# Loading the weight sums earlier, and two moved steps in the mixer, in a two-layer hybrid decoder

## The chip, the cores and the metric

The kernel runs on one NeuronCore of a Trainium2 chip. The metric is the device time of one execution in microseconds (us). The engines are TensorE (PE, matrix products; its weight loads are listed as PEld), VectorE (DVE), ScalarE (ACT), GpSimd (POOL) and SyncE (SP, which here only issues DMAs).

## The reference

The program computes a decoder trunk of two layers for 256 tokens of width 2048, all in float32. Layer 0 mixes with one input projection whose columns feed an mLSTM group (8 heads) and a Mamba-2 SSD group (32 heads); layer 1 is attention with rotary positions (with 256 tokens there is one block, so only the causal part is left). Each layer ends in a SwiGLU feed-forward part with 5632 hidden columns.

```
for layer in range(2):
    xn = rms_norm(x, norm_mix[layer])
    x = x + (mixer_mlstm_ssd if layer == 0 else mixer_moba)(xn, ...)
    x = x + swiglu(rms_norm(x, norm_ffn[layer]), gate, up, down)
return rms_norm(x, final_norm)

# mLSTM part of the mixer, per head, after the chunks are put together:
#   num = (q k^T * decay) v ; nq = its row sums ; hm = num / max(|nq|, exp(-m))
#   hm  = rms_norm(hm) * sigmoid(o)
```

## The kernel before

**Products.** Every large product is a `block`: 256 tokens (two tiles of 128) by two strips of 512 output columns, summed over pairs of 128 input rows. Pair j of a block covers 256 rows. Each float32 number is split into a high and a low part, so that one product becomes three matmuls (`add`, lines 303 to 305): high times high, high times low, low times high. The letter of a plan says how a pair is done. P is the plain way, 8 products of 3 matmuls. S is Strassen's way with 7 products, 3 matmuls each, for which sums of weights and of activations are needed. PPPSPSSP, for instance, has S at pairs 3, 5 and 6. It is the plan of the blocks `v0`, `o` (twice), `qk1`, `v1`, both halves of `w2` and nearly all of layer 1's projections; most hidden blocks of the feed-forward part have PSPSPSSP.

**Weights.** `weights` (line 251) loads a pair's raw weights through SP (lines 262, 264, 266; 512 KB or 256 KB each) into one of six `raw` buffers, which hold three pairs. For an S pair it also fills a `sums` tile, one of two buffers: two plain loads of 256 KB on SP (line 260), then two accumulating loads on POOL (line 261), each of which has to wait for its plain load. Then ACT casts the high parts (line 270, `wh`, six buffers) and DVE takes the low parts (line 275, `wl`, six buffers) and two more sums (lines 285 and 287). An S pair has four casts: its first raw tile, `sums`, the second raw tile, and half of a fourth tile. The casts are tied to each other in the order of the program (`last`, `cast`) and stand at high priority (offset 800).

**Order.** The program is written as a stream; a planner then puts each engine's instructions into a fixed order, by priority (the place in the program, or earlier with `high_priority`) among what it reckons to be ready, including free buffers. On the chip every engine runs its own list in order and waits at an instruction whose inputs are not there. `tied(x)` (lines 151 to 155) puts what is traced in it behind instruction `x` on `x`'s engine. `issued` collects the first raw load of each pair, so `issued[-2]` at pair j is that of pair j - 2, since pair j's own is added afterwards.

**Later work.** Small steps between the products are put into a list by `later(wait, name, fn, ...)` and run at a `tick`, one at the end of each pair of a block; `wait` counts ticks. From the first S pair on the ticks are held back until the last S pair is through, so that in PPPSPSSP only the ticks behind pairs 0, 1 and 2, and then the one behind pair 7, run such steps. `need(name)` runs what is left under a name. Steps that come up at one tick run in the order in which they were put into the list. The auxiliary results go to the PSUM banks 7, 6, 4, 5 in turn (`aux_bank`); the same four banks hold the `acc_e` sums of the S pairs, and the first of these that a pair writes is in bank 4.

**The mixer.** After the query-key block `qk0` and the first output projection `w1` come `v0`, `o0`, and the second half, `qk1`, `v1`, `o1`, then the output projection `w2` in two halves. `qk_done` turns queries and keys with `qk_pair` (eight transposes each time, four times). `mlstm_scores` multiplies them by the decays (line 803 on DVE). In the output-gate block `o`, `mlstm_out` (products `p_num`, line 814, and copies on ACT, line 817) and `mlstm_norm` (squares on ACT, a power on POOL, scaling on ACT) run for two groups of heads, `s` = 2g and 2g + 1. At the end of the block line 851 on DVE multiplies the gate in, and `transpose_split` (line 215) turns the result, `p_tr<-ident,pre`, one block later. In layer 1 the rotary products (lines 981 to 987) and their transposes `p_qt<-ident,rot` (line 770) stand in the same relation.

## Time and profile before

| what | value |
|---|---|
| median of 3 runs | 2567.66 us (2567.1 to 2573.02) |
| the profiled execution's own time | 2568.26 us |
| its span | 2566.5 us |
| mean granted clock of PE | 0.995 |
| PE busy | 2535.6 us, 99% |
| DVE busy | 2237.1 us, 87% |
| ACT busy | 1600.2 us, 62% |
| POOL busy | 366.2 us, 14% |
| read from HBM | 627.07 MB, 245 GB/s over the span |

Busy shares are of the span. Matmuls are pipelined, so that a busy PE is not PE at its best pace. A group's row names line, engine, operation, out<-in, count, then busy time and the mean of one in ns, then the engine's idle time just before and what ended it. Lines ending in `q` after the engine's name are of its sequencer, for SP the issue of a DMA. All times within the span are in us from its start.

### The profile page before, as it was taken

How to read it: one execution, taken by the hardware profiler on the slowest of the kernel's cores; microseconds unless marked ns; L12 is line 12 of the kernel's file. 1: busy time of each engine (PE TensorE's matmuls, PEld its weight loads, DVE VectorE, ACT ScalarE, POOL GpSimd, SP SyncE). 2: the span in 40 equal slices, each digit the busy share in tenths (PEclk: the TensorE clock that was granted, in tenths of full speed). 3: DMA queues.
4: the chain of work that ended last, by engine and by line, in shares of the span. 5: the costliest groups of instructions: out<-in, count | busy, mean ns of one | idle time of the engine just before them, and what ended most of it. 6: DMA issues, size and time to landing. Idle time of an engine off the chain costs nothing.

```text
span 2566.5 us, 34451 instructions
## 1 busy us (share of the span) xinstructions
PE 2535.6 (99%) x11553; PEld 2088.3 (81%) x11553; DVE 2237.1 (87%) x2978; ACT 1600.2 (62%) x2160; POOL 366.2 (14%) x452
## 2 busy tenths in 40 slices
PE   9999999999999999999999999999999999999998
PEld 8888888878778888888888887778888888888887
DVE  6877788778789999999999988878899999999998
ACT  6566765566667665566666665656666656665665
POOL 2101111111101111111111010110011111111110
PEclk9999999999999999999999999999999999999999
DMA  8656678778768999999999887785699999999995
GB/s 281 182 172 182 212 205 257 222 220 248 225 200 261 275 274 279 280 275 273 273 291 273 253 240 212 227 233 179 192 266 273 279 282 269 285 262 293 288 267 179
DMA packets 333665, 631.51 MB, mean 246 GB/s; under 512 B 27256, under 2 KB 29824, under 8 KB 333488
## 3 DMA queue, kind: packets, MB, share of 16 engines
q1 hardware_dynamic: 278928, 527.71, 60.9%
q0 software_dynamic: 53376, 99.76, 22.7%
q8 instruction: 91, 1.49, 0.2%
q10 hardware_dynamic: 1184, 1.84, 0.2%
q14 instruction: 86, 0.70, 0.1%
HBM read 627.07 MB, written 2.14 MB: 245 GB/s over the span
## 4 chain that ended last, share of the span: by engine, by line
PE 71%; DVE 3%; DMA 2%; ACT 1%; issue 1%; POOL 0%; POOLq 0%; DVEq 0%; ACTq 0%; SPq 0%
PE acc_f L303 17%; PE acc_f L305 17%; PE acc_f L304 17%; PE acc_e L303 6%; PE acc_e L305 5%; PE acc_e L304 5%; DVE wl L275 2%; PE p_tr L215 1%; DMA sums<-in_l_w_qkv 1%; ACT wh L270 1%; DMA sums<-in_l_w_in 1%; PE p_qt L770 0%; DMA raw<-in_l_ffn_down 0%; DMA sums<-in_l_w_out 0%; PE p_o L1038 0%
## 5 line engine op out<-in xcount | busy, mean ns | idle before, releaser
L270 ACT CAST wh<-raw 128x1024 fp32r<-128x1024 f32 (+1 forms) x1084 | 1047.0, 982 | 597.7 <-PE acc_f L305 272.0
L275 DVE TENSOR_TENSOR wl<-raw,wh 128x1024 fp32r<-128x1024 f32 (+1 forms) x1084 | 1210.6, 1135 | 180.1 <-ACT wh L270 163.4
L303 PE MATMUL acc_f<-wh,x 128*128 128x512 f32 x1168 | 458.4, 392 | 0.0
L304 PE MATMUL acc_f<-wl,x 128*128 128x512 f32 x1168 | 457.8, 392 | 0.0
L305 PE MATMUL acc_f<-wh,x 128*128 128x512 f32 x1168 | 457.8, 392 | 0.0
L270 ACT CAST wh<-sums 128x1024 fp32r<-128x1024 f32 x174 | 183.0, 1052 | 199.1 <-PE acc_f L305 83.6
L303 PE MATMUL acc_f<-wh,xa 128*128 128x512 f32 x678 | 269.6, 398 | 0.7 <-ACT wh L145 0.7
L304 PE MATMUL acc_f<-wl,xa 128*128 128x512 f32 x678 | 264.8, 390 | 1.1 <-DVE wl L275 1.1
L305 PE MATMUL acc_f<-wh,xa 128*128 128x512 f32 x678 | 264.9, 391 | 0.0
L304 PEld LDWEIGHTS acc_f<-wl,x 128*128 128x128 f32 x1168 | 220.3, 189 | 45.0
L303 PEld LDWEIGHTS acc_f<-wh,x 128*128 128x128 f32 x1168 | 220.3, 189 | 44.8
L305 PEld LDWEIGHTS acc_f<-wh,x 128*128 128x128 f32 x1168 | 220.0, 188 | 45.1
L275 DVE TENSOR_TENSOR wl<-sums,wh 128x1024 fp32r<-128x1024 f32 x174 | 212.1, 1219 | 43.5 <-ACT wh L270 43.1
L303 PE MATMUL acc_e<-wh,sk 128*128 128x512 f32 x522 | 206.7, 396 | 0.1
L304 PE MATMUL acc_e<-wl,sk 128*128 128x512 f32 x522 | 204.0, 391 | 0.0
L305 PE MATMUL acc_e<-wh,sk 128*128 128x512 f32 x522 | 202.8, 390 | 0.0
L261 POOL DMA_DIRECT2D sums<-in_l_ffn_gate x86 | 74.4, 865 | 726.5 <-DMA sums<-in_l_ffn_up 278.2
L304 PEld LDWEIGHTS acc_f<-wl,xa 128*128 128x128 f32 x678 | 127.5, 188 | 27.4 <-DVE wl L275 1.9
L305 PEld LDWEIGHTS acc_f<-wh,xa 128*128 128x128 f32 x678 | 127.3, 188 | 27.1
L303 PEld LDWEIGHTS acc_f<-wh,xa 128*128 128x128 f32 x678 | 127.4, 188 | 25.7 <-ACT wh L145 0.9
L285 DVE TENSOR_TENSOR raw<-raw,sums 128x512 f32<-128x512 f32 x174 | 119.0, 684 | 25.9 <-DMA sums<-in_l_w_qkv 8.6
L261 POOL DMA_DIRECT2D sums<-in_l_ffn_down x80 | 69.9, 946 | 380.0 <-DMA sums<-in_l_ffn_down 204.0
(336 smaller groups left out, 4111.7 us busy)
## 6 DMA issues: line engine op xcount, KB each, us to landing
raw<-in_l_w_in SPq DMA_DIRECT2D x177, 512.0 KB, 4.4
raw<-in_l_ffn_gate SPq DMA_DIRECT2D x176, 512.0 KB, 6.1
raw<-in_l_ffn_down SPq DMA_DIRECT2D x136, 512.0 KB, 6.6
raw<-in_l_ffn_up SPq DMA_DIRECT2D x90, 512.0 KB, 6.4
sums<-in_l_ffn_up SPq DMA_DIRECT2D x172, 256.0 KB, 5.3
raw<-in_l_w_qkv SPq DMA_DIRECT2D x78, 512.0 KB, 5.0
raw<-in_l_w_out SPq DMA_DIRECT2D x52, 512.0 KB, 5.1
raw<-in_l_ffn_up SPq DMA_DIRECT2D x86, 256.0 KB, 5.9
```

What stands on the lines that cost most here:

```text
L215: turned = nc.tensor.transpose(pt[:, i * T + t * P:i * T + (t + 1) * P], src[t][:, i * P:(i + 1) * P], ident)
L261: nc.gpsimd.dma_start(sums[:, i, :], other, accum_op=OP.add)
L270: cast[0] = nc.scalar.copy(h[:, :n, :], of[:, :n, :]).ins
L275: last[0] = nc.vector.tensor_sub(l[:, :n, :], of[:, :n, :], h[:, :n, :].bitcast(F32)).ins
L285: nc.vector.tensor_add(b[:, 1, :], b[:, 0, :], sums[:, 0, :])
L303: nc.tensor.matmul(dst, ah, bh, start=start, stop=False, **kw)
L304: nc.tensor.matmul(dst, ah, bl, start=False, stop=False, **kw)
L305: nth[0] = nc.tensor.matmul(dst, al, bh, start=False, stop=stop, **kw).ins
```

## The change

The loads of a pair's `sums` are tied to the first raw load five pairs back in place of two. Where the query-key block has S pairs (`qk1`), all four `qk_pair` steps come up at the second tick; before, the queries came up at the first and the keys at the second. In the second output-gate block (g = 1) `mlstm_out` comes up at ticks 2 and 3 (before: 1 and 2), and `mlstm_norm` twice at tick 3 (before: 2 and 3). With g = 0 nothing changes there.

```
@@ weights
         if summed:
             sums = home("sum")([P, 2, STRIP], "sums")
-            with tied(issued[-2]):
+            with tied(issued[-5]):
                 for i, other in enumerate((unit(wa, row + P, ca), unit(wb, row, cb))):
                     nc.sync.dma_start(sums[:, i, :], unit(wb, row + P, cb))
                     nc.gpsimd.dma_start(sums[:, i, :], other, accum_op=OP.add)
@@ qk_done
             for j in range(2):
-                later(1 + i, ("qk", g), qk_pair, qk[g, i][:, 2 * j:2 * j + 2, :],
+                later(1 + i if got[1] is None else 2, ("qk", g), qk_pair, qk[g, i][:, 2 * j:2 * j + 2, :],
                       [tok[i, t][:, j * T:(j + 1) * T] for t in range(NT)])
@@ o_block
         for i in range(2):
-            later(1 + i, ("hm", g), mlstm_out, 2 * g + i)
-            later(2 + i, ("hm", g), mlstm_norm, 2 * g + i)
+            later(1 + g + i, ("hm", g), mlstm_out, 2 * g + i)
+            later(min(2 + g + i, 3), ("hm", g), mlstm_norm, 2 * g + i)
```

## The prediction

> **What bounds the kernel now.** I read the page first, for the span and the busy shares. TensorE (PE) is busy for nearly the whole span, so a change of the loading order can only win the moments in which PE stands idle or runs at a reduced clock. To find them I asked for the busy time in stretches, cut at the blocks of the mixer of layer 0 and of the projections of layer 1, which are the consecutive blocks with the plan PPPSPSSP.

> ```profile
> span 2566.5 us, 34451 instructions
> ```

> ```profile
> core 0: us, PE busy (x) PEld busy (x) DVE busy (x) ACT busy (x) POOL busy (x), PEclk, DMA share, GB/s
> 497.00:543.00 46.00, 44.16 (x191) 35.25 (x190) 29.05 (x42) 29.77 (x55) 5.53 (x6) 1.00 0.68 193
> 543.00:592.00 49.00, 45.65 (x202) 37.13 (x201) 40.21 (x50) 32.71 (x48) 8.61 (x13) 0.97 0.85 251
> ...
> 637.00:687.00 50.00, 48.97 (x219) 40.29 (x218) 35.54 (x50) 33.90 (x60) 7.30 (x9) 1.00 0.74 214
> 687.00:738.00 51.00, 45.93 (x187) 36.30 (x186) 38.72 (x56) 29.25 (x40) 4.85 (x6) 0.90 0.64 187
> ...
> 1556.00:1606.00 50.00, 46.16 (x207) 37.75 (x206) 42.22 (x58) 27.60 (x41) 5.24 (x6) 0.97 0.73 211
> 1606.00:1659.00 53.00, 51.17 (x245) 41.52 (x245) 46.35 (x73) 33.04 (x60) 5.23 (x6) 1.00 0.71 206
> 1659.00:1707.00 48.00, 46.92 (x219) 38.74 (x218) 36.31 (x51) 29.85 (x48) 5.27 (x6) 1.00 0.77 222
> 1707.00:1756.00 49.00, 46.47 (x209) 37.97 (x208) 42.42 (x59) 26.60 (x40) 5.20 (x6) 0.97 0.75 218
> sum 529.00, PE 508.44 PEld 415.50 DVE 421.68 ACT 325.89 POOL 63.25; mean PE 46.22 PEld 37.77 DVE 38.33 ACT 29.63 POOL 5.75
> ```

> The first two numbers of a row are its length and PE's busy time; the last three the granted clock, the DMA share and GB/s. The rows are, in order, the first output-gate block (o0), the second query-key block (qk1), the second output-gate block (o1), the first half of the last mixer projection (w2a), and in layer 1 aq1, av1, aq2 and aq3. The sum row covers eleven stretches: 529.00 - 508.44 = 20.56 us idle, and the eight quoted rows hold all of it (1.84, 3.35, 1.03, 5.07, 3.84, 1.83, 1.08, 2.53). Four rows show a clock below 1.00.

> The chain of waits tells what PE stood for in qk1 (start, length, what).

> ```profile
> 545.15 9.08 DMA sums<-in_l_w_in
> 554.33 1.05 ACT wh L270
> 555.41 1.23 DVE wl L275
> 556.63 0.60 DVE raw L287
> 557.24 1.21 DVE pre L851 x2
> 558.49 3.48 PE p_tr L215 x15
> ```

> An accumulating load of `sums` of pair 3 (S) lands at 554.23; ScalarE (ACT) then casts it, VectorE (DVE) takes the low part, and only then comes to L851, the gate of the block before, for which PE's transposes wait. PE did not wait for weights: it waited for other work queued on DVE behind the late `sums`. The waits and PE's groups say the same of the other blocks.

> ```profile
> ACT wh L270 <- PE acc_f L305: 355.7, 246, 6.4
> ...
> ACT wh L270 <- DMA sums<-in_l_w_in: 18.9, 4, 6.6
> ...
> ACT wh L270 <- DMA sums<-in_l_w_qkv: 14.8, 3, 6.0
> ...
> ACT wh L270 <- DMA sums<-in_l_w_out: 7.9, 2, 5.3
> ```

> ```profile
> L814 PE MATMUL p_num<-v,rows 128*128 128x257 f32 x48 | 11.5, 383 | 1.0 <-DVE rows L803 1.0
> L1038 PE MATMUL p_o<-pT,av 128*128 128x256 f32 x32 | 9.8, 389 | 1.8 <-DVE prob L1012 1.8
> L770 PE MATMUL p_qt<-ident,rot 128*128 128x128 f32 x64 | 9.8, 285 | 6.4 <-DVE rot L987 6.4
> ...
> L215 PE MATMUL p_tr<-ident,pre 128*128 128x128 f32 x32 | 7.3, 379 | 6.3 <-DVE pre L851 6.3
> ```

> The last numbers are PE's idle time before the group. 6.4 us of p_qt are aq1 and aq3 (3.84 + 2.53), 6.3 of p_tr are qk1 and 2.95 of w2a's 5.07, p_o's 1.8 is av1, p_num's 1.0 is o1. All wait for small DVE operations, in blocks where `sums` came late by 5 to 7 us at worst. The first waits row says that casts mostly wait for PE to give buffers back: weights are otherwise ahead.

> **Part 1, the tie of the sums.** Nothing is added or removed; two loads on SP and two accumulating loads on POOL per S pair may be issued earlier. Is there a free buffer? There are two, taken in turn, so pair 3 gets the one of pair 5 of the block before, which is free after that pair's low part.

> ```profile
> 527.18 1.22 DVE L275 TENSOR_TENSOR wl<-sums,wh 128x1024 fp32r<-128x1024 f32 x1
> ```

> ```profile
> 529.56 0.37 SPq L262 DMA_DIRECT2D raw<-in_l_w_in  x1
> ...
> 538.22 0.92 SPq L260 DMA_DIRECT2D sums<-in_l_w_in  x2
> ...
> 541.06 0.39 SPq L260 DMA_DIRECT2D sums<-in_l_w_in  x1
> ```

> The buffer is free at 528.40 but its loads go out at 538.22, behind the raw loads of pairs 0 to 2; the old tie is to pair 1. The new one is to pair 6 of the block before, long issued. I expect the loads at about 528.4, just ahead of raw pair 0 at 529.56: 538.22 - 528.40 = 9.8 us earlier, in a stretch with little in flight. From issue to landing it took 554.23 - 538.22 = 16.0 us; from 528.4 that is 544.4. The chain's 6.6 us longest wait is then gone, since the wait ran up to 554.33 and so began at 547.7, later than 544.4. L851 ends 6.6 us earlier, 558.45 - 6.6 = 551.9, before PE comes to its transposes (3.35 us idle before about 558.5, so 555): the whole stall goes. The same shift of 5 to 6 us in w2a, aq1 and aq3 exceeds their stalls of 2.95, 3.84 and 2.53, so these go too, and with them the 1.83 of av1 and 1.08 of aq2. Pair 5 moves from 541.06 to ahead of raw pair 1. Pair 6 waits for pair 3's buffer and not for the tie, so it only follows pair 3. On POOL each accumulation waits for its SP load to land; behind it in that queue stand the memset of v and the power operations, which no PE group above waits for, so I put this at 0.

> A stall also costs clock.

> ```profile
> 498.06 0.39 PE L304 MATMUL acc_f<-wl,xa 128*128 128x512 f32 x1
> 498.29 0.39 PE L305 MATMUL acc_f<-wh,xa 128*128 128x512 f32 x1
> ```

> ```profile
> 704.35 0.63 PE L304 MATMUL acc_f<-wl,mx 128*128 128x512 f32 x1
> 704.78 0.63 PE L305 MATMUL acc_f<-wh,mx 128*128 128x512 f32 x1
> ```

> Matmuls start 0.23 us apart before a stall and 0.43 after it. From the clock column, 0.03 x 49 + 0.10 x 51 + 0.03 x 50 + 0.03 x 49 = 9.5 us of full clock are withheld. What falls into the idle itself costs nothing, so the loss is 0 to 9.5; I take 7, near the top, since the slow starts come after the idle. [...]

> Ceiling: 20.6 + 7 = 27.6 us. Not all is due to late sums. The rest of w2a's idle, 5.07 - 2.95 = 2.1, lies later in the block, and o0's 1.84 is at S pairs behind normalising work on ACT; earlier sums give ACT room, and I take half of each (0 to all): 1.05 and 0.9 stay.

> **What is pushed back.** Raw pairs 1 and 2 now come behind pair 5's sums, 1 MB of reads in all. At the 251 GB/s of qk1 that is 4.2 us at most, in eight blocks 34 us if all of it reached PE; the other end is 0. I take 0, because PE is not near its weights there: the first waits row has 246 casts waiting for PE, while the sums rows have 9 waits. If that cover were gone, each us that raw pair 1 is later than the lead would be a us of PE idle.

> In the feed-forward blocks (PSPSPSSP) the buffers bind pairs 1, 5 and 6, and only pair 3 moves, from behind raw pair 1 to ahead of it.

> ```profile
> 860.20 0.39 SPq L260 DMA_DIRECT2D sums<-in_l_ffn_up  x1
> ```

> ```profile
> 864.61 1.06 ACT L270 CAST wh<-raw 128x1024 fp32r<-128x1024 f32 x1 [0.46 <-DMA raw<-in_l_ffn_gate]
> ```

> ```profile
> 867.91 1.22 DVE L275 TENSOR_TENSOR wl<-raw,wh 128x1024 fp32r<-128x1024 f32 x1
> ```

> There raw pair 1 is cast the moment it lands, so 0.5 MB ahead of it (about 2 us at 251 GB/s) delays the cast by 0 to 2 us. DVE takes it up at 867.91, 2.2 us after the cast ends at 865.67: covered. I take 0.

> **Part 2, queries and keys of qk1 at one tick.** Eight transposes and two ACT copies go from behind pair 0 of v1 to behind pair 1. The scores need them only after pair 2, and v1 stood without idle, since the eight quoted rows hold all idle of the sum. Cost 0; at worst the scores wait for the two extra copies.

> **Part 3, heads of o1 a pair later.** The products of s = 2 go behind pair 1, those of s = 3 behind pair 2, directly ahead of S pair 3; both normalisations come at pair 2's tick. PE's 1.03 us wait for L803 goes (in the ceiling already). New is that `acc_e` of pair 3 takes bank 4, which the products of s = 3 have just filled: its second product, three matmuls or 0.7 us after them, waits for ACT's copies.

> ```profile
> 653.46 2.76 PE L814 MATMUL p_num<-v,rows 128*128 128x257 f32 x12
> ```

> ```profile
> 656.42 1.18 ACT L817 COPY v<-p_num 128x257 f32<-128x257 f32 x4
> ...
> 660.29 1.03 ACT L270 CAST wh<-raw 128x1024 fp32r<-128x1024 f32 x1
> ```

> The four copies take 1.18 us after the products (653.46 + 2.76 = 656.22), so this wait is 0 to 1.2 on a free ACT, and up to 3.9 if copies and squares (656.42 to 660.29) stand before it; I take 1. The cast of pair 4 stands behind the squares of s = 3, which are now a pair later: 0 to 3.9, I take 1.5, like o0's 1.84. Together 2.5 us lost. POOL's small power operation of each normalisation stands behind pair 6's accumulations, as now; these come earlier with pair 3.

> Sum: 27.6 - 1.05 - 0.9 - 2.5 = 23.2 us. The profiled execution took 2568.26; 2568.26 - 23.2 = 2545.1. The median of the runs, 2567.66, is 0.6 lower, which I leave aside: 2545.

> **The rivals.** (a) Raw loads take the sums' place.

> ```profile
> raw<-in_l_w_in SPq DMA_DIRECT2D x177, 512.0 KB, 4.4
> ```

> An accumulation of 256 KB took 9.08 us where a raw load of 512 KB takes 4.4: loads in company are slow. If raw pairs 1 and 2 become as late as the accumulations (4.7 us), DVE waits there, and about half the shift is lost: 12 us gained, 2556. For it: DMA is at 0.85 in qk1; against: casts wait for PE. [...]

> (b) The order does not move. The planner goes by program order when slots are free in its own reckoning; if it still puts pair 3's sums behind raw pair 2, only part 3 acts, +2.5 - 1.0: about 2570. Against it: the sums at 541.06 already go out ahead of raw loads that stand before them in the program.

> (c) Slower. In the 20 hidden blocks of the feed-forward with the plan PSPSPSSP raw pair 1 comes so late that PE waits. If PE loses all of the 2 us, 40 us go against 23 gained: 2585. It decides from 23 / 20 = 1.2 us a block. Against it: DVE takes the cast up only 2.2 us later, as shown.

> **How the numbers follow.** Forecast (2536 to 2553) 0.65; (a) 0.13; (b) 0.12; (c) 0.10. About 0.3%, 7.7 us, is what a measurement here can tell from no change, so faster means below 2560: 0.65 + 0.10 of (a) = 0.75; the same: 0.03 + 0.12 = 0.15; slower: 0.10. The range 2536 to 2564 leaves out (c), half of (b) and 0.04 below. Its low end is the full ceiling with 9.5 for the clock, 2568.3 - 30.1 = 2538, and 2 us beside.

> **What would show it.** SP issues pair 3's sums ahead of raw pair 0; ACT's waits for sums of w_in, w_qkv and w_out fall from 41.6 us to a few; p_tr<-pre and p_qt<-rot lose their 6.3 and 6.4 us of idle; the four clock values return to 1.00; o1 shows a short wait of `acc_e` for ACT L817. The prediction is wrong if ACT's or DVE's waits for raw rise by as much, or if PE shows new idle in the feed-forward.

## The result and the profile after

The changed kernel takes 2549.89 us, the median of four runs, against 2567.38 us for the kernel before on the same chip: ratio 0.9925, 95% interval 0.9906 to 0.9945. (One of the four, at 3621 us with a granted clock of 0.654, was disturbed; the other three took 2548.43 to 2550.68, median 2549.11, and the ratio leaves it out.) The time lies inside the predicted range, about 5 us above the predicted 2545. The profiled execution took 2548.43.

```profile
span 2546.7 us, 34498 instructions
```

The span is 2566.5 - 2546.7 = 19.8 us shorter. The stretches of the prediction, cut at the same blocks (o0, qk1, o1, w2a, aq1, av1, aq2, aq3; PE's busy time, then clock, DMA share and GB/s at the end):

```profile
core 0: us, PE busy (x) PEld busy (x) DVE busy (x) ACT busy (x) POOL busy (x), PEclk, DMA share, GB/s
500.00:546.00 46.00, 46.00 (x206) 38.35 (x205) 33.74 (x46) 31.48 (x57) 7.87 (x8) 1.00 0.73 214
546.00:595.00 49.00, 47.81 (x218) 39.18 (x217) 42.84 (x54) 35.83 (x52) 8.37 (x12) 1.00 0.92 275
640.00:690.00 50.00, 50.00 (x223) 41.63 (x222) 36.20 (x50) 32.95 (x59) 7.33 (x8) 1.00 0.74 216
690.00:741.00 51.00, 47.41 (x216) 37.73 (x215) 45.13 (x65) 33.59 (x51) 5.24 (x6) 1.00 0.77 220
...
sum 396.00, PE 391.22 PEld 321.50 DVE 337.38 ACT 259.62 POOL 46.34; mean PE 48.90 PEld 40.19 DVE 42.17 ACT 32.45 POOL 5.79
```

The sum covers eight rows; the four not shown are those of layer 1, where PE is busy throughout. Of the 20.56 us idle in these blocks 396.00 - 391.22 = 4.78 are left: 1.19 in qk1 and 3.59 in w2a. Every row grants the full clock. That makes 20.56 - 4.78 = 15.8 us of idle gone, and with it up to 9.5 us of withheld clock. The sum, 25.3, is more than the span lost, so something else was paid. It stands in PE's groups, where each group's last numbers are its idle time and what ended it:

```profile
L814 PE MATMUL p_num<-v,rows 128*128 128x257 f32 x48 | 11.0, 380 | 0.0
L1038 PE MATMUL p_o<-pT,av 128*128 128x256 f32 x32 | 9.7, 384 | 0.0
L770 PE MATMUL p_qt<-ident,rot 128*128 128x128 f32 x64 | 9.4, 277 | 0.0
L699 PE MATMUL p_xs<-ident,xs 128*128 128x128 f32 x32 | 5.4, 294 | 5.6 <-DVE xs L481 5.6
L215 PE MATMUL p_tr<-ident,pre 128*128 128x128 f32 x32 | 5.2, 285 | 2.7 <-DVE pre L851 2.7
```

The 1.0 us at p_num, 1.8 at p_o and 6.4 at p_qt are gone, and the 6.3 at p_tr<-pre are 2.7. But PE now waits 5.6 us at L699, the transposes of the last x-z block, which run during qk0 (the first query-key block). The stretch around that wait:

```profile
326.00:345.00 19.00, 13.37 (x63) 11.00 (x63) 16.76 (x33) 10.90 (x20) 1.80 (x2) 0.91 0.78 218
```

19.00 - 13.37 = 5.6 us of idle and 0.09 x 19 = 1.7 us of withheld clock: 7.3 us lost. The balance 25.3 - 7.3 = 18.0 stands against the measured 19.8; I did not follow the other 1.8 us.

**What is late at L699.** In the list of waits in the changed kernel (us in all, times, longest):

```profile
DVE rows L659 <- DMA rows<-scr: 5.8, 2, 5.6
...
POOL rows L655 <- DMA sums<-in_l_w_out: 2.4, 2, 1.3
```

VectorE waits at L659 for eight loads of `rows` (L655, the decay rows of the state-space heads), which POOL issues. POOL's own rows in order of time, first before:

```profile
307.55 5.92 POOL L655 DMA_DIRECT2D rows<-scr  x8
```

and after:

```profile
312.25 1.83 POOL L261 DMA_DIRECT2D sums<-in_l_w_out  x2 [4.58 <-DMA sums<-in_l_w_out]
313.98 4.42 POOL L655 DMA_DIRECT2D rows<-scr  x6
319.48 0.71 POOL L655 DMA_DIRECT2D rows<-scr  x1 [1.08 <-DMA sums<-in_l_w_out]
321.52 0.71 POOL L655 DMA_DIRECT2D rows<-scr  x1 [1.34 <-DMA sums<-in_l_w_out]
```

The first mixer projection, w1, has the plan PSPSPSPP. Its first S pair is pair 1, so the fifth load back is the raw load of pair 4 of qk0, and SP issues its sums at 307.25, where before it was

```profile
324.39 1.37 SPq L260 DMA_DIRECT2D sums<-in_l_w_out  x2
```

POOL's two accumulations wait 4.58 us for their plain loads, and behind them in that queue stand the rows: issued from 313.98 in place of 307.55, the last at 321.52 in place of about 313. The chain of waits shows the rest:

```profile
307.25 4.43 DMA sums<-in_l_w_out
...
313.14 0.93 POOL sums L261
314.08 0.64 POOL rows L655
314.72 8.05 DMA rows<-scr
...
332.40 0.69 DVE xs L481
333.23 1.09 PE p_xs L699 x4
```

VectorE waits 5.65 us for the rows, works off its backlog, and reaches L481 at 332.40; PE has been waiting since 327.6.

**What is late in qk1 now.** The issue order there is as the prediction said: sums of pair 3 ahead of raw pair 0, sums of pair 5 ahead of raw pair 1.

```profile
531.09 0.82 SPq L260 DMA_DIRECT2D sums<-in_l_w_in  x2
532.23 0.38 SPq L262 DMA_DIRECT2D raw<-in_l_w_in  x1
...
536.42 0.86 SPq L260 DMA_DIRECT2D sums<-in_l_w_in  x2
537.56 0.56 SPq L262 DMA_DIRECT2D raw<-in_l_w_in  x1
```

ScalarE's casts in order of time, before:

```profile
546.74 1.04 ACT L270 CAST wh<-raw 128x1024 fp32r<-128x1024 f32 x1
554.33 1.05 ACT L270 CAST wh<-sums 128x1024 fp32r<-128x1024 f32 x1 [6.55 <-DMA sums<-in_l_w_in]
```

and after (the first row is the cast of pair 2's second raw load, the second that of pair 3's raw load):

```profile
550.48 1.06 ACT L270 CAST wh<-raw 128x1024 fp32r<-128x1024 f32 x1 [1.34 <-DMA raw<-in_l_w_in]
...
553.29 1.03 ACT L270 CAST wh<-raw 128x1024 fp32r<-128x1024 f32 x1
554.23 1.05 ACT L270 CAST wh<-sums 128x1024 fp32r<-128x1024 f32 x1
```

Here ScalarE no longer waits for sums, but the sums are cast at nearly the same moment: the raw cast ahead of them, begun at 546.74 before, now begins at 553.29, 6.55 us later. Most of this is not due to the loads. In the block ahead of qk1 the first `acc_e` matmul of pair 5 begins at 528.18 before and at 533.46 after, so that all of qk1 comes 5.3 us later (the 7.3 us lost at L699, less some 2 us won in o0). What is left, about 1.3 us, is the size of the wait for the raw load in the first row. How much of this reaches PE, and which loads cause it, this place alone does not say. The experiments do.

### The profile page after: what moved, and what is told of

It is laid out like the page before. It is cut to its first block, busy times and chain, and to the rows that moved or that the text cites. A ratio compares the mean times of both kernels' runs of the same rounds, so it can differ in the third digit from the quotient of the medians.

```text
span 2546.7 us, 34498 instructions
## 1 busy us (share of the span) xinstructions
PE 2525.5 (99%) x11553; PEld 2083.3 (82%) x11553; DVE 2237.2 (88%) x2978; ACT 1601.3 (63%) x2160; POOL 366.8 (14%) x452
## 3 DMA queue, kind: packets, MB, share of 16 engines
q10 hardware_dynamic: 1184, 1.84, 0.2%
## 4 chain that ended last, share of the span: by engine, by line
PE 95%; DVE 3%; DMA 1%; issue 1%; ACT 0%; POOL 0%; SPq 0%; POOLq 0%; DVEq 0%; ACTq 0%
PE acc_f L303 24%; PE acc_f L305 24%; PE acc_f L304 24%; PE acc_e L303 6%; PE acc_e L305 6%; PE acc_e L304 6%; PE p_tr L215 2%; DVE wl L275 1%; PE p_y L725 1%; PE p_qt L770 0%; PE p_num L814 0%; DMA raw<-in_l_ffn_down 0%; ACT wh L270 0%; DMA rows<-scr 0%; PE p_o L1038 0%
## 5 line engine op out<-in xcount | busy, mean ns | idle before, releaser
L270 ACT CAST wh<-raw 128x1024 fp32r<-128x1024 f32 (+1 forms) x1084 | 1049.5, 982 | 644.4 <-PE acc_f L305 283.8
L275 DVE TENSOR_TENSOR wl<-raw,wh 128x1024 fp32r<-128x1024 f32 (+1 forms) x1084 | 1211.3, 1135 | 189.2 <-ACT wh L270 177.4
L305 PE MATMUL acc_f<-wh,x 128*128 128x512 f32 x1168 | 456.8, 391 | 0.0
L304 PE MATMUL acc_f<-wl,x 128*128 128x512 f32 x1168 | 456.8, 391 | 0.0
L270 ACT CAST wh<-sums 128x1024 fp32r<-128x1024 f32 x174 | 183.0, 1052 | 149.8 <-PE acc_f L305 87.4
L305 PE MATMUL acc_f<-wh,xa 128*128 128x512 f32 x678 | 265.1, 391 | 0.0
L304 PE MATMUL acc_f<-wl,xa 128*128 128x512 f32 x678 | 264.8, 391 | 0.0
L305 PEld LDWEIGHTS acc_f<-wh,x 128*128 128x128 f32 x1168 | 219.4, 188 | 44.9
L304 PEld LDWEIGHTS acc_f<-wl,x 128*128 128x128 f32 x1168 | 219.5, 188 | 44.7
L275 DVE TENSOR_TENSOR wl<-sums,wh 128x1024 fp32r<-128x1024 f32 x174 | 212.1, 1219 | 27.3 <-ACT wh L270 26.9
L304 PE MATMUL acc_e<-wl,sk 128*128 128x512 f32 x522 | 203.6, 390 | 0.0
L305 PE MATMUL acc_e<-wh,sk 128*128 128x512 f32 x522 | 202.7, 390 | 0.0
L305 PEld LDWEIGHTS acc_f<-wh,xa 128*128 128x128 f32 x678 | 127.5, 188 | 27.2
L304 PEld LDWEIGHTS acc_f<-wl,xa 128*128 128x128 f32 x678 | 127.8, 189 | 25.7 <-DVE wl L146 0.4
L303 PEld LDWEIGHTS acc_f<-wh,xa 128*128 128x128 f32 x678 | 127.6, 188 | 25.9 <-ACT wh L145 1.0
L303 PEld LDWEIGHTS acc_e<-wh,sk 128*128 128x128 f32 x522 | 98.0, 188 | 29.4 <-ACT xg L226 6.8
## 6 DMA issues: line engine op xcount, KB each, us to landing
raw<-in_l_w_in SPq DMA_DIRECT2D x177, 512.0 KB, 4.7
raw<-in_l_ffn_gate SPq DMA_DIRECT2D x176, 512.0 KB, 6.2
raw<-in_l_ffn_down SPq DMA_DIRECT2D x136, 512.0 KB, 7.1
raw<-in_l_ffn_up SPq DMA_DIRECT2D x90, 512.0 KB, 6.5
raw<-in_l_w_qkv SPq DMA_DIRECT2D x78, 512.0 KB, 6.4
raw<-in_l_w_out SPq DMA_DIRECT2D x52, 512.0 KB, 5.9
```

The lines of the kernel that those rows point to most:

```text
L270: cast[0] = nc.scalar.copy(h[:, :n, :], of[:, :n, :]).ins
L275: last[0] = nc.vector.tensor_sub(l[:, :n, :], of[:, :n, :], h[:, :n, :].bitcast(F32)).ins
L303: nc.tensor.matmul(dst, ah, bh, start=start, stop=False, **kw)
L304: nc.tensor.matmul(dst, ah, bl, start=False, stop=False, **kw)
L305: nth[0] = nc.tensor.matmul(dst, al, bh, start=False, stop=stop, **kw).ins
```

## The experiments

All ratios are to the kernel before, run beside each group of kernels on the same chip. The groups ran on several chips, and the median of the kernel before lay between 2567 and 2572 us in them, so ratios are the safer comparison across groups.

**Which part brings the gain.** Two kernels: part 1 alone, and parts 2 and 3 alone.

```
part 1 alone:       qk_done, o_block as before; tied(issued[-5])
parts 2 and 3 alone: qk_done, o_block as changed; tied(issued[-2])
```

> Part 1 alone (sums tied to the fifth load back); the heads of the second output-gate block and the turning of queries and keys stand where they stood before. Theory A, the tie carries the whole change: 2549 to 2552 us, with PE's waits for L851 and for L987 as in the changed kernel, and at most the 1.0 us wait of p_num for L803 back in the second output-gate block. Rival, the moved heads and turns give VectorE and ScalarE the room that the tie needs: 2555 us or more, with stalls of over 1 us back in the second query-key or second output-gate block.

> Parts 2 and 3 alone, with the old tie of the sums. Theory A: within 3 us of the time before, 2565 to 2570 us: the stalls of 3.35 us in the second query-key block, 5.07 in the last mixer projection, and 3.84 and 2.53 in layer 1 all stand, only the 1.0 us of the second output-gate block can go. Rival: 2562 us or less, since heads and turns at other ticks free VectorE where the sums come late.

Part 1 alone: 2549.13 us, ratio 0.9917 (0.9903 to 0.9930). Parts 2 and 3 alone: 2569.03, ratio 0.9995 (0.9984 to 1.0006). The tie carries the change; the moves are worth nothing that can be measured. The 1.0 us of p_num is gone with part 1 alone, and also with parts 2 and 3 alone, so either of the two is enough to take that wait away.

**The loss at L699: three ways to take it away.** First the old tie for w1 only, so that its sums are not issued early at all:

```
-            with tied(issued[-5]):
+            with tied(issued[-2 if wa is w_out and row >= D else -5]):
```

> The changed kernel, but the sums of the first mixer projection (the lower half of w_out) keep the old tie. Theory B, the queue of POOL: the changed kernel's new wait of 5.6 us before the transposes p_xs at L699 comes from two accumulations of that projection which stand on POOL ahead of the eight loads of rows at L655; with the old tie the rows land in time, the wait is gone with the 1 us of half clock behind it, and the time is 2543 to 2544 us. Rival: VectorE, busy for the whole of that stretch, is late by its own work or by the raw loads, and the wait stays or moves: 2548 to 2551 us.

2543.73 us, ratio 0.9899 (0.9885 to 0.9912). No wait at L699; POOL's first row of `rows` is at 307.69 again. This takes away the early traffic with the queue's order, so it can't tell the two apart. The second way was to issue the rows from SP:

```
-            nc.gpsimd.dma_start(rb[:, :, lo:lo + n],
+            nc.sync.dma_start(rb[:, :, lo:lo + n],
```

> The changed kernel, but all loads of rows at L655 are issued by SP in place of POOL, where no accumulation stands ahead of them. Theory B, the queue of POOL alone makes the rows late: PE's wait of 5.6 us at p_xs and the half clock behind it go, though the sums are loaded just as early, and the time is 2543 to 2546 us. Rival, the early sums delay the rows and raw loads by their traffic, or DVE by its own work: the wait stays at 3 us or more, 2547 to 2551 us.

2550.36 us, ratio 0.9924 (0.9906 to 0.9942): a miss, the time is the rival's. The wait shrank but others came, at the same transposes of the earlier x-z blocks, which had none before:

```profile
PE p_xs L699 <- DVE xs L481: 3.9, 4, 1.6
```

These 3.9 us are less than the 6.6 us by which this kernel is slower than the one with the old tie for w1; the rest was not followed. On SP the rows stand among raw loads and go out late as well:

```profile
313.84 1.95 SPq L655 DMA_DIRECT2D rows<-scr  x4
315.89 0.43 SPq L262 DMA_DIRECT2D raw<-in_l_w_in  x1
316.37 3.10 SPq L655 DMA_DIRECT2D rows<-scr  x4
```

One late queue was changed for another, so a third kernel turned round nothing but POOL's order: SP's loads stand as in the changed kernel, row by row, and the accumulations are issued behind the eight loads of rows.

```
+            rowed.append(nc.gpsimd.dma_start(rb[...], ...).ins)
...
-                    nc.gpsimd.dma_start(sums[:, i, :], other, accum_op=OP.add)
+                    with tied(*(rowed[-8:] if wa is w_out and row >= D else ())):
+                        nc.gpsimd.dma_start(sums[:, i, :], other, accum_op=OP.add)
```

> The changed kernel with one order turned round on POOL: the accumulating loads of the first mixer projection's sums are issued behind the eight loads of rows at L655 of the last x-z block; SP's loads, the early plain loads of these sums among them, keep their order. It settles what the run with rows on SP left open, since there the rows only changed one late queue for another. Theory B, POOL's queue order is the whole loss: PE's 5.6 us at p_xs and the half clock behind it go although the traffic is early, 2542 to 2545 us, as with the old tie for that projection (2543.7). Rival, early plain loads of 256 KB beside the raw loads make rows or raw pair 6 late: 2 us or more of wait at p_xs stays, 2546 to 2550 us.

2544.72 us, ratio 0.9898 (0.9881 to 0.9914). POOL's rows are in the old place, and the stretch has no idle left:

```profile
307.77 0.74 POOL L655 DMA_DIRECT2D rows<-scr  x1
308.67 5.03 POOL L655 DMA_DIRECT2D rows<-scr  x7 [0.15 <-issue]
314.26 0.93 POOL L261 DMA_DIRECT2D sums<-in_l_w_out  x1 [0.57 <-DMA rows<-scr]
```

```profile
326.00:339.00 13.00, 13.00 (x74) 11.18 (x73) 12.21 (x25) 7.99 (x13) 1.74 (x2) 1.00 0.93 284
```

That settles it: the early plain loads do no harm there; the harm comes from the accumulations' place on POOL's queue, ahead of the rows. The spans of this kernel and of the one with the old tie for w1 are 2544.3 and 2542.4 us, 2.4 and 4.3 below the changed kernel's and not the whole 7.3. Part of the difference is the clock in w2a, first with POOL's order turned round, then with the old tie:

```profile
682.00:733.00 51.00, 46.93 (x196) 37.18 (x195) 42.14 (x62) 31.74 (x44) 5.23 (x6) 0.93 0.76 214
```

```profile
683.00:734.00 51.00, 47.49 (x204) 37.60 (x203) 43.11 (x63) 32.18 (x47) 5.24 (x6) 0.97 0.75 214
```

For 4.07 and 3.51 us of idle 0.07 x 51 = 3.6 and 0.03 x 51 = 1.5 us of clock are withheld, where the changed kernel, with 3.59 us, kept 1.00.

**Are pair 5's early sums the reason for what is left in qk1 and w2a?** The long tie for the first S pair of a block only:

```
-def weights(src, row, summed):             with tied(issued[-5]):
+def weights(src, row, summed, back=5):     with tied(issued[-back]):
...
-    ... = weights(src, row + 2 * j * P, True)
+    ... = weights(src, row + 2 * j * P, True, 5 if j == first_s else 2)
```

> The changed kernel, but only the first S pair of a block is tied to the fifth load back; the other S pairs keep the old tie, so pair 5's sums go out behind raw pair 2 or 3 again. Theory C, pair 5's early sums take the place of raw loads (raw pair 3 of the second query-key block landed 7 us later than before): its 1.7 us and the 2.2 us at the first transposes of the last mixer projection go, and part of the 5.6 us at p_xs, as only two of the four early accumulations are left ahead of the rows: 2543 to 2547 us. Rival, early sums of pair 5 are themselves part of the gain: stalls at L987 or in the value blocks of layer 1 come back, and the time is 2550 to 2556 us.

2546.50 us, ratio 0.9904 (0.9891 to 0.9918), and the two places are empty:

```profile
L770 PE MATMUL p_qt<-ident,rot 128*128 128x128 f32 x64 | 9.3, 276 | 0.0
L699 PE MATMUL p_xs<-ident,xs 128*128 128x128 f32 x32 | 5.4, 294 | 5.9 <-DVE xs L481 5.9
...
L215 PE MATMUL p_tr<-ident,pre 128*128 128x128 f32 x32 | 4.3, 276 | 0.1
```

p_tr<-pre falls from 2.7 to 0.1 us and nothing comes back at p_qt. So the earliness of pair 5 had no use, and its early loads had made the raw loads late (over the run ScalarE waits for them at L270 for 92.5 us in the changed kernel and 35.6 us here). (Plain and accumulating loads moved together here, so this run does not say which of them did it.) The part of my expectation that half of the early accumulations would mean a smaller wait at L699 was wrong: 5.9 us in place of 5.6. The two accumulations that are left already hold up the queue: POOL waits 4.40 us for their plain loads, and the rows begin at 313.93, where they began at 313.98 with all four early.

**Both corrections together**, and then with the feed-forward or the moves left as before:

```
both:             back = 2 in w1; 5 for the first S pair of other blocks; else 2
feed-forward old: weights(..., 5 if j == first_s == 3 else 2)
moves old:        as both, with qk_done and o_block as before
```

> The changed kernel with both corrections: the first mixer projection keeps the old tie, and in all other blocks only the first S pair is tied to the fifth load back. If the two losses (7.3 us of extra PE time between 327 and 345 us in the changed kernel, 1.7 and 2.2 us in the second query-key block and the last mixer projection) are separate, the gains add up: the run with only the first S pairs early had 8.7 us of extra PE time at p_xs left, so 2546.5 - 8.7 = 2537.8 us, 2536 to 2540. Rival: with no stall at p_xs the later blocks begin earlier and meet their loads less well, and a part comes back there: 2541 to 2544 us.

> As the run with both corrections, and the feed-forward blocks whose first S pair is pair 1 keep the old tie too. The prediction's cost of nothing for the feed-forward: the same time as with both corrections, within 3 us. Rival, the early sums of pair 1 and pair 3 cost raw loads there: 3 to 8 us faster than with both corrections. Other rival, the feed-forward gains from them: 3 us or more slower.

> As the run with both corrections, but the heads of the second output-gate block and the turning of queries and keys stand where they stood before. The prediction put the heads at 2.5 us lost against 1.0 us of a wait gained, so 1 to 2 us faster than with both corrections, or the same within 2 us if, as the changed kernel's trace has it, no wait of acc_e for L817 arises. Rival, the moved heads are of use once the sums are on time: 2 us or more slower.

Both: 2539.70 us, ratio 0.9879 (0.9859 to 0.9898); feed-forward old: 2538.45, 0.9874 (0.9854 to 0.9893); moves old: 2538.46, 0.9875 (0.9855 to 0.9895). The losses were separate and the gains add up. The three can't be told apart, so the moved heads and turns cost nothing and bring nothing that can be measured. On the feed-forward the run with it left old says little: SP issues its loads in the same order as with both corrections, but for two places in the down projections (in the first of them sums go out at 1405.05 in place of 1400.00). Pair 1's tie decides almost nothing there, and pair 3, the one that the prediction saw move, is early in neither kernel.

**The least change, and how early is early enough.** One line against the kernel before: only where pair 3 is the first S pair are its sums tied to the fifth load back; then the same with the third load back, so that raw pair 0 goes first.

```
-    ... = weights(src, row + 2 * j * P, True)
+    ... = weights(src, row + 2 * j * P, True, 5 if j == first_s == 3 else 2)     (3 in place of 5)
```

> One line against the kernel before: the sums of pair 3 are tied to the fifth load back where pair 3 is the first S pair of its block; every other tie, the heads and the turning of queries and keys stand as before. If these early sums alone carry the gain, the time is that of the three runs with both corrections, 2537 to 2541 us. Rival: leaving out the moves and the feed-forward together costs what each alone did not show, 2542 us or more.

> As the run with the sums of pair 3 alone early, but tied to the third load back in place of the fifth: they go out behind raw pair 0 of their block and ahead of pairs 1 and 2. Theory D, what counts is that they land before ScalarE reaches them, 6 to 7 us earlier than before the change: two raw loads earlier is enough, 2537 to 2542 us. Rival, each place in the queue counts, since the accumulation starts only when the plain load has landed in company of the raw loads: a third to a half of the stalls at L851 and L987 is back, 2546 to 2555 us.

Fifth: 2539.37 us (2538.98 to 2539.89), ratio 0.9875 (0.9859 to 0.9892). Third: 2542.03 (2540.59 to 2543.10), ratio 0.9886 (0.9871 to 0.9900). The first is as fast as any and beats the changed kernel's 0.9925 (its interval begins at 0.9906). Behind raw pair 0 nearly all of the gain is still there (the time is at the upper end of what was expected, 0.03 us outside); the groups of the second kernel show what the 2.7 us are in part:

```profile
L215 PE MATMUL p_tr<-ident,pre 128*128 128x128 f32 x32 | 4.7, 280 | 1.3 <-DVE pre L851 1.3
```

where the first has 0.1.

## Why the prediction was right, and where it was not

The direction, the cause and most of the size held. That the total came out within 5 us of the forecast is in part luck: two steps that were put at 0 lost 10.0 us (7.3 and 2.7) and the rest of w2a another 1.05, while terms that were too cautious gave 5.9 us back (2.5 in o1, 2.5 of clock, 0.9 in o0).

- **The late sums were the cause.** Held. ScalarE has no wait for sums of w_in, w_qkv or w_out left in the list of waits, where it had 41.6 us; p_qt, p_o and p_num lost all of their idle, p_tr<-pre 3.6 of 6.3 us.
- **The loads' place.** Held: pair 3's sums ahead of raw pair 0, pair 5's ahead of raw pair 1. SP issues pair 3's at 531.09, as soon as DVE is through with the low part that held the buffer (529.85 + 1.22 = 531.07).
- **POOL at 0.** This step failed. The prediction named what stands behind a hoisted accumulation as "the memset of v and the power operations" and so left out qk0. The rows loads of L655 in qk0 stand there too, ahead of w1's sums. It cost 7.3 us, and the turned order on POOL takes it away.
- **What is pushed back, at 0.** This failed in part. Rival (a), raw loads in the sums' place, came true in two of eight blocks: the 2.7 us of p_tr<-pre are 1.19 in qk1 and 1.5 of w2a's 3.59. With pair 5 not early, they go to 0.1. In the trace of before a raw load of 512 KB issued at 534.89 landed after 3.8 us, and one issued at 548.22, beside the accumulations, after 9.4. That casts wait for PE over the run as a whole did not protect the two blocks in which loads were short. One sign that the prediction named for its being wrong did come. ScalarE's waits for raw loads at L270 rose by 55.6 us, more than the 41.6 that the waits for sums lost: from 36.9 (ffn_gate 18.3, ffn_down 15.4, w_in 3.2) to 92.5 (ffn_gate 25.9, w_in 10.5, w_out 9.7, ffn_up 2.1 and the two rows here):

```profile
ACT wh L270 <- DMA raw<-in_l_ffn_down: 28.3, 10, 3.7
...
ACT wh L270 <- DMA raw<-in_l_w_qkv: 16.0, 15, 3.0
```

With only the first S pair of a block early they are 35.6 us again. So raw loads did land later nearly wherever sums went ahead of them, but of all these waits little more than the 2.7 us at p_tr<-pre shows as idle of PE: elsewhere PE still had work in hand.
- **o0 and w2a's rest, half of each.** o0's 1.84 went wholly, so 0.9 was too cautious. The later stall of w2a stayed in full, also in the fastest kernels: there PE waits for ScalarE's casts, and earlier sums do not help.
- **o1's new waits, 2.5 us.** They did not come. The products end at 657.76 + 2.76 = 660.52, the copies follow them closely, and `acc_e` starts at 661.04:

```profile
657.76 2.76 PE L814 MATMUL p_num<-v,rows 128*128 128x257 f32 x12
661.04 0.39 PE L303 MATMUL acc_e<-wh,xa 128*128 128x512 f32 x1
```

```profile
659.91 1.18 ACT L817 COPY v<-p_num 128x257 f32<-128x257 f32 x4
```

ScalarE begins copying before the products end, so the copies end at 661.09, 0.6 us after them, about the time of the three matmuls between; the row of before had the copies begin after the products.
- **Clock, 7 of 9.5.** All eight blocks are back at 1.00, so 9.5 was nearer. In the new stall the clock fell again, 0.91 over 19 us.
- **Feed-forward and part 2 at 0.** Both held. For the feed-forward the changed kernel's trace shows it, since pair 3's sums are early there: in the block of the prediction they go out at 850.60, ahead of raw pair 1 at 851.97, where before they went out at 860.20, behind raw pair 1 at 858.68. In the 676 us of the first feed-forward (784 to 1460 before, 777 to 1453 after) PE is idle for 0.06 us before and 0.37 after; in 710 us of the second (1850 to 2560, 1830 to 2540) for 2.09 and 1.92. For part 2 the run without the moves shows it: it differs from the one with both corrections by 1.2 us, within the intervals. Rivals (b) and (c) did not come.

With 20.6 + 9.5 - 4.8 - 7.3 the terms give 18.0 us, as against 23.2 forecast and 19.8 measured in the profiled span; the 1.8 us between them stay open.

## What to carry to other kernels

When a load is moved ahead, list what every queue that it uses issues between the new place and the old, in each block that the rule reaches: an accumulating load waits on POOL's queue for its plain load (here 4.58 us) and holds up the loads behind it (here the rows, by 6.4 us). Move only the load that is late: here the sums of pair 3 alone, one line for sixteen blocks, gave 2539 us, where moving all sums gave 2550. A busy share or a count of waits over the whole run says little of the two blocks that run short, and a rise of ScalarE's waits by 55.6 us cost PE hardly more than 2.7 us of idle. A variant tests a step only if it changes the order of the loads that the step is about: the one with the feed-forward left old hardly did.

## What the runs showed of the hardware that I had not expected

POOL's queue holds in order across unrelated loads: six loads of rows were issued 6.4 us later (313.98 against 307.55) because two accumulations ahead of them waited 4.58 us for their plain loads; with only POOL's order turned round, and SP's as it was, the rows began at 307.77 again. At that place loads of 256 KB that were early did no harm by their traffic: with POOL's order turned round, the stretch from 326 to 339 us moved 284 GB/s and PE was busy throughout. And about the same idle cost different amounts of clock: w2a kept 1.00 with 3.59 us of idle in the changed kernel, and was granted 0.97 and 0.93 with 3.51 and 4.07 us in two others, in pieces whose order in the block is the same.

```profile
707.59:711.00 3.41, 1.69 (x5) 0.78 (x5) 2.28 (x6) 1.87 (x3) 1.75 (x2) 1.00 0.72 214
711.00:714.42 3.42, 3.42 (x10) 2.69 (x9) 1.94 (x3) 0.00 (x0) 0.00 (x0) 0.51 0.85 196
```

```profile
711.51:714.93 3.42, 2.64 (x11) 1.63 (x9) 3.38 (x7) 1.13 (x2) 0.00 (x0) 1.00 0.61 167
714.93:718.34 3.41, 2.08 (x8) 1.30 (x9) 2.31 (x5) 1.57 (x2) 1.75 (x2) 1.00 0.79 214
718.34:721.75 3.41, 3.41 (x17) 2.77 (x16) 1.86 (x3) 1.89 (x2) 0.00 (x0) 1.00 1.00 226
```

The same three waits fall almost wholly into one stretch in the first trace, where PE is busy for 1.69 of 3.41 us and the next stretch is granted 0.51. In the second a boundary splits them, PE is busy for 2.64 and 2.08 us, and the clock stays at 1.00. PE's busy time in a stretch does not decide alone either. At the later stall of w2a in the trace of before, 1.83 us were followed by 0.50; at the stall at L699 in the changed kernel, 1.81 us were followed by 1.00, and only the stretch behind that one, with PE idle throughout, by 0.50:

```profile
718.43:721.84 3.41, 1.83 (x6) 0.66 (x4) 2.78 (x7) 1.18 (x2) 0.00 (x0) 1.00 0.42 140
721.84:725.25 3.41, 2.88 (x7) 2.30 (x8) 2.43 (x3) 1.00 (x2) 0.00 (x0) 0.50 0.45 168
```

```profile
325.78:329.19 3.41, 1.81 (x8) 1.13 (x7) 3.41 (x9) 2.21 (x5) 0.00 (x0) 1.00 0.96 288
329.19:332.61 3.42, 0.00 (x0) 0.00 (x0) 3.42 (x6) 2.62 (x7) 1.80 (x2) 1.00 0.77 186
332.61:336.02 3.41, 2.79 (x9) 2.44 (x10) 3.41 (x8) 2.02 (x4) 0.00 (x0) 0.50 1.03 238
```

How little PE must do in a stretch for the next to be slow was not measured.
